# A late S5 input, the tables' transfers on GpSimd's queue and four background steps behind a pair, in a 9-stage fp32 network

## The chip, the cores and the metric

One NeuronCore of a Trainium2 chip runs the whole program. The metric is the device time of one execution in microseconds (us).

## What is computed

A small network runs over 512 tokens of 1024 channels in fp32. The first block has a pooling mixer, a conv-GeGLU layer, windowed attention and a second conv-GeGLU layer, each with a norm ahead of it and one behind. The second block has an S5 mixer and a Mamba-like SSD mixer, each with an MLP behind it. Their inputs are normed and modulated by vectors that come from a condition `c`. In short:

```python
def second_block(x, c, ...):                  # after first_block: pool, ffn, attention, ffn
    ada = silu(c) @ ada_w[i] + ada_b[i]       # six vectors: shift, scale, gate, twice
    h = rmsnorm(x, norm_mix_g) * (1 + scale) + shift
    x = x + gate * s5_mixer(h, ...)           # layer 0; layer 1 has the SSD mixer
    ...                                       # and each layer an MLP, of the same form

def s5_mixer(h, w_in, lam, log_dt, b, c, d, w_glu, b_glu):
    u = h @ w_in
    s_t = exp(lam * dt) * s_(t-1) + b_bar @ u_t          # complex, by group of 16 channels
    y = (c_mat @ s_t).real + d * u
    val, gate = split(gelu(y) @ w_glu + b_glu)
    return val * sigmoid(gate)
```

## The kernel before, in words

The residual `x` lies transposed in SBUF: `xT[k]`, k from 0 to 7, is 128 channels by 512 tokens. Every fp32 product is made of three products of halves: an operand is split into a rounded part (`hi`, or `wh` of a weight) and a remainder (`lo`, `wl`), and lines 218 to 220 add `hi*wh`, `lo*wh` and `hi*wl` in PSUM. ScalarE makes the rounded parts (L203 for weights), VectorE the remainders (L204). Weights come through three buffers `ws`, loaded from SP's queue.

The layers stand in the order pool, ffn0, attn, ffn1, s5, mlp0, ssd, mlp1 and a final norm. Two layers meet in `seam` (L785). For each half of the tokens (256 each) it runs the tail of the old layer, then its chain: `post_add` (L427) makes the post-norm, whose squares are summed on TensorE (`pn`, L303), turned to a root on ScalarE (`sr`, L305), to a reciprocal on VectorE, and spread over all partitions by a second product (L312). `u` (L434) and `x` (L437) follow on VectorE. A step of the new `x`'s squares goes to ScalarE and VectorE (L294, L295).

The new layer's own norm comes in two forms. `PreNorm` runs inside the seam for each half: it waits for all squares of the new `x`, makes the statistics (L303 to L312 again), then `u`, the rounded `h` and its remainder (L388 to L392). `PreScale` is the late form: `h` is the split of `x` times a gain, by `parts` in the same staged loop as `u` and `x` (L418, L419), and the products of the layer are multiplied by the norm's reciprocal root `rs` when they leave PSUM. The two conv-GeGLU layers use `PreScale`, the S5 layer uses `PreNorm` with gain `gs` = (1 + scale) times the weight of the norm, and the shift as an addend. Then the new layer's head computes its first products half by half, and its body the rest over all 512 tokens. In the S5 layer these are `u = h @ w_in`; `u_out` (L1331) copies each from PSUM, permuted, into `usc`, from where it goes through DRAM into `U`.

While a conv-GeGLU layer runs, a `Background` object (L1834) advances generators: `rate` steps behind each of ten pairs of columns, and one behind each of 16 evacuations of the down-projection. What is left is drained behind the body. In ffn0 (rate 5) it computes the tables of the S5 layer (`s5_tables`, `s5_mats`): per group of channels loads `bs` and `cs`, small products on all engines, stores to DRAM (`d_tab`, `d_k`). In ffn1 (rate 3) it computes the condition's vectors by `vecmat` (L466), a vector times a 1024 by 6144 matrix on VectorE: each of 12 blocks of 512 columns takes eight loads `as` of 256 KB into two buffers, one multiply and seven multiply-adds `aa` (L486, L488), then three bf16 parts `ab` by ScalarE with two subtractions between (L498), summed on TensorE. Beside it `s5_toeplitz` reads `d_k` back in shifted form (`tz`, 64 loads), permutes it on ScalarE (`th`, L775, one buffer) and stores it. In the S5 body, `ct` (1 MB each, two buffers) and `vt` (through GpSimd's queue) hold the tables; `dec` and `xs` are small steps on GpSimd.

A scheduler turns the program into an order for each engine; it decides which of the steps above come first on an engine. DMAs are issued in order too: each queue (SP, GpSimd, ScalarE) waits with the first until its buffer is free, and what stands behind it waits as well. `psm` PSUM banks are four, the norm's `psn` one.

## Time and profile before

| what | value |
|---|---|
| median of 3 runs (lowest, highest) | 2488.61 us (2488.39, 2492.14) |
| profiled execution | 2485.38 us |
| its span, first to last instruction | 2483.7 us |
| mean granted TensorE clock | 0.972 |
| busy: TensorE, VectorE, ScalarE, GpSimd | 94%, 69%, 46%, 14% |
| chain that ended last: TensorE, VectorE, DMA, ScalarE, issue | 74%, 12%, 6%, 4%, 3% |

The page shows busy times of the engines as an average over stages. A table by stretch of time then shows where TensorE is not busy, and the timeline of one engine what it waited for there: a row's bracket gives the idle time ahead of an instruction and what ended it. PE is TensorE, DVE is VectorE, ACT is ScalarE, POOL is GpSimd, SP is the queue of SyncE. Line numbers are those of the kernel before.

### The profile page before, as it was taken

To read this page: it belongs to the slowest core of one execution; us is meant where nothing else is said; L and a number is where in the kernel's file an instruction comes from. 1 tells how busy PE (TensorE), PEld (TensorE's weight loads), DVE (VectorE), ACT (ScalarE), POOL (GpSimd) and SP (SyncE) were. 2 spreads that over 40 slices of the span, in tenths; PEclk is the share of its full clock that TensorE was granted. 3 is DMA by queue.
4 is the path that set the end of the run, shared out by engine and by line. 5 is a ranking of instruction groups with operands and counts; after the bars stand their busy time and mean duration, and the time that the engine had idled before them with its cause. 6 is when DMAs were issued, how large, how long until landed. Compare 5 with 4: busy or idle time off the path is not lost.

```text
span 2483.7 us, 33557 instructions
## 1 busy us (share of the span) xinstructions
PE 2340.7 (94%) x12397; PEld 1972.1 (79%) x12397; DVE 1713.8 (69%) x3069; ACT 1142.1 (46%) x2038; POOL 337.9 (14%) x345
## 2 busy tenths in 40 slices
PE   7999999788979999986899999999999999999998
PEld 7877777776778888875878887889878888888888
DVE  6896989678658778786655666666777788633333
ACT  6543535467665444344543433334555554422332
POOL 1001223201200000000110210110143331200110
PEclk9999999889989999997999999999999999999999
DMA  4224443311274555552942455543433332232222
GB/s 122 88 88 140 131 142 103 125 52 51 75 206 134 180 178 165 179 173 68 306 153 77 143 166 191 188 134 92 125 105 99 107 104 80 93 102 94 95 88 72
DMA packets 297780, 311.29 MB, mean 125 GB/s; under 512 B 53569, under 2 KB 251025, under 8 KB 296593
## 3 DMA queue, kind: packets, MB, share of 16 engines
q1 hardware_dynamic: 270033, 278.22, 36.0%
q10 hardware_dynamic: 23680, 17.31, 2.3%
q0 software_dynamic: 3904, 13.63, 1.7%
q8 instruction: 97, 1.59, 0.3%
q14 instruction: 66, 0.54, 0.1%
HBM read 284.92 MB, written 24.18 MB: 124 GB/s over the span
## 4 chain that ended last, share of the span: by engine, by line
PE 74%; DVE 12%; DMA 6%; ACT 4%; issue 3%; SPq 0%; POOL 0%; DVEq 0%; ACTq 0%; POOLq 0%
PE mm L219 22%; PE mm L218 22%; PE mm L220 22%; DMA as<-in_ada_w 3%; DVE wl L204 3%; ACT wh L203 1%; DVE aa L488 1%; PE mm L1642 1%; PE mm L1643 1%; PE mm L1644 1%; PE pb L1712 1%; PE pb L754 1%; DMA tz<-d_k 1%; ACT th L775 1%; DMA d_u<-usc 1%
## 5 line engine op out<-in xcount | busy, mean ns | idle before, releaser
L218 PE MATMUL mm<-h,wh 128*128 128x512 f32 (+1 forms) x1792 | 665.6, 374 | 22.9 <-ACT h L418 7.2
L219 PE MATMUL mm<-h,wh 128*128 128x512 f32 (+1 forms) x1792 | 666.1, 372 | 6.2 <-DVE h L392 3.3
L220 PE MATMUL mm<-h,wl 128*128 128x512 f32 (+1 forms) x1792 | 664.8, 372 | 1.7 <-DVE wl L204 1.7
L203 ACT ACTIVATE wh<-ws 128x1024 fp32r<-128x1024 f32 (+1 forms) x367 | 388.0, 1060 | 563.3 <-PE mm L219 479.6
L204 DVE TENSOR_TENSOR wl<-ws,wh 128x1024 fp32r<-128x1024 f32 (+1 forms) x367 | 466.0, 1272 | 240.7 <-ACT wh L203 234.3
L218 PEld LDWEIGHTS mm<-h,wh 128*128 128x128 f32 x1792 | 346.8, 194 | 81.0 <-issue 8.5
L219 PEld LDWEIGHTS mm<-h,wh 128*128 128x128 f32 x1792 | 347.1, 194 | 63.3 <-DVE h L392 5.4
L220 PEld LDWEIGHTS mm<-h,wl 128*128 128x128 f32 x1792 | 347.3, 194 | 56.3 <-DVE wl L204 2.5
L218 PE MATMUL mm<-hi,wh 128*128 128x512 f32 (+1 forms) x1056 | 369.5, 354 | 9.0 <-ACT wh L203 7.6
L219 PE MATMUL mm<-lo,wh 128*128 128x512 f32 (+1 forms) x1056 | 372.0, 353 | 1.7 <-DVE lo L319 1.7
L220 PE MATMUL mm<-hi,wl 128*128 128x512 f32 (+1 forms) x1056 | 370.8, 353 | 0.8 <-DVE wl L204 0.8
L218 PEld LDWEIGHTS mm<-hi,wh 128*128 128x128 f32 x1056 | 200.6, 190 | 37.3 <-ACT wh L203 8.7
L219 PEld LDWEIGHTS mm<-lo,wh 128*128 128x128 f32 x1056 | 201.4, 191 | 28.5 <-DVE lo L319 2.7
L220 PEld LDWEIGHTS mm<-hi,wl 128*128 128x128 f32 x1056 | 201.2, 191 | 26.8 <-DVE wl L204 1.0
L488 DVE SCALAR_TENSOR_TENSOR aa<-as,cond,aa 128x512 f32<-128x512 f32 x168 | 132.0, 786 | 113.8 <-DMA as<-in_ada_w 112.3
L1266 POOL TENSOR_TENSOR r<-r 128x512 f32<-128x512 f32 x64 | 88.1, 1379 | 671.1 <-ACT r L1262 488.0
L760 POOL TENSOR_TENSOR dd<-ident,s5dg 16x64 f32<-16x64 f32 x16 | 69.4, 4337 | 343.1 <-DVE kt L762 336.1
L319 DVE TENSOR_TENSOR lo<-r,hi 128x512 fp32r<-128x512 f32 x64 | 48.1, 756 | 76.5 <-ACT hi L317 76.4
L1287 DVE SCALAR_TENSOR_TENSOR x<-mm,mod,x 128x512 f32<-128x512 f32 (+1 forms) x76 | 48.9, 662 | 60.6 <-PE mm L220 60.4
L496 ACT ACTIVATE ab<-aa 128x512 bf16<-128x512 f32 x72 | 44.9, 624 | 97.0 <-DVE aa L488 61.7
L317 ACT ACTIVATE hi<-r 128x512 fp32r<-128x512 f32 x64 | 40.4, 631 | 72.3 <-POOL r L1266 72.3
L295 DVE TENSOR_TENSOR acc<-acc,sq 128x256 f32<-128x256 f32 (+1 forms) x148 | 62.0, 432 | 16.4 <-ACT sq L294 11.6
(484 smaller groups left out, 3651.2 us busy)
## 6 DMA issues: line engine op xcount, KB each, us to landing
ws<-in_mlp_w SPq DMA_DIRECT2D x124, 512.0 KB, 4.0
as<-in_ada_w SPq DMA_DIRECT2D x192, 256.0 KB, 3.1
ws<-in_ffn_w_in SPq DMA_DIRECT2D x88, 512.0 KB, 3.8
ws<-in_m_w_in SPq DMA_DIRECT2D x41, 512.0 KB, 3.7
ws<-in_ffn_w_out SPq DMA_DIRECT2D x40, 512.0 KB, 3.5
ws<-in_w_o SPq DMA_DIRECT2D x16, 512.0 KB, 3.4
ct<-d_tab SPq DMA_DIRECT2D x8, 1024.0 KB, 9.5
ws<-in_s_w_glu SPq DMA_DIRECT2D x16, 512.0 KB, 5.8
```

The costliest lines, as they stand in the source:

```text
L203: A.activation(h_, s_, AF.Copy)
L204: V.tensor_tensor(l_, s_, f(h_), ALU.subtract)
L218: T.matmul(ps, wh, xh, start=first, stop=False)
L219: T.matmul(ps, wh, xl, start=False, stop=False)
L220: return T.matmul(ps, wl, xh, start=False, stop=last).ins
L295: V.tensor_tensor(dst, dst, sq[:, a:b], ALU.add)
L319: return hi_, V.tensor_tensor(lo[:, ts], src, f(hi[:, ts]), ALU.subtract)
L488: V.scalar_tensor_tensor(acc, st, col(k), acc, ALU.mult, ALU.add)
L496: A.activation(parts[j], acc, AF.Copy)
L760: G.tensor_tensor(dd, ident[:16, :16].unsqueeze(1).broadcast_to([16, 4, 16]), dg[:, g4].unsqueeze(2).broadcast_to([16, 4, 16]), ALU.mult)
L1266: G.tensor_tensor(r, r, r, ALU.mult)
L1287: V.scalar_tensor_tensor(xT[n][:, ts], ps, md(i, 5, n), xT[n][:, ts], ALU.mult, ALU.add)
```

## The change

1. The S5 layer takes the late input: `PreScale` with the modulated gain. `u_out` multiplies the product by `rs` on VectorE (a new tile `us`) and adds `s5c`, the shift times `w_in`, as the bias of ScalarE's permuting copy. `s5c` is made by a second `vecmat` of two blocks behind the twelve, with its parts permuted as the columns of `w_in` are.
2. These DMAs are issued by GpSimd in place of SP: the `as` loads of layer 0 (96) and of the new product (16 more), the stores `ph` (16) and of zeros to `d_k` (8), the loads `bs` and `cs` (32 each), `tz` (64) and `ct` (8).
3. The second conv-GeGLU layer advances four background steps behind a pair, in place of three.

Two constants of the norms now share a tile.

```diff
     class PreNorm:
...
-            i, m, gname = modulate
-            self.gs = cst.tile([P, KD], F32, tag="gs", bufs=2, name=nm("gs"))
-            c = i * 48 + (m + 1) * 8
-            go = voff[gname] + 8 * i
-            V.scalar_tensor_tensor(self.gs, mod[:, c:c + 8], 1.0, vec[:, go:go + 8], ALU.add, ALU.mult)
+            self.gs = modulated(*modulate)
...
     class PreScale(PreNorm):
-        def __init__(self, norm, eps, gain=None):
-            self.norm, self.eps, self.gain = norm, eps, gain
+        def __init__(self, norm, eps, gain=None, modulate=None):
+            self.norm, self.eps = norm, eps
+            if modulate is not None:
+                gs = modulated(*modulate)
+                self.gain = lambda k: gs[:, k:k + 1]
+            else:
+                self.gain = lambda k: 1.0 if gain is None else vc(gain[0], gain[1] + k)
...
-    def vecmat(pool, W, ncb, col, done):
+    def vecmat(pool, W, ncb, col, done, perm=False, queue=nc.gpsimd):
...
-                nc.sync.dma_start(st, W[k * P:(k + 1) * P, cb * 512:(cb + 1) * 512])
+                queue.dma_start(st, W[k * P:(k + 1) * P, cb * 512:(cb + 1) * 512])
...
+            pv, av = parts, acc
+            if perm:
+                pv = [p_.rearrange("p (a h g) -> p a h g", h=16, g=8) for p_ in parts]
+                av = acc.rearrange("p (a g h) -> p a h g", g=8, h=16)
             for j in range(3):
-                A.activation(parts[j], acc, AF.Copy)
+                A.activation(pv[j], av, AF.Copy)
                 if j < 2:
-                    V.tensor_tensor(acc, acc, parts[j], ALU.subtract)
+                    V.tensor_tensor(av, av, pv[j], ALU.subtract)
...
-        yield from vecmat(pool, I["ada_w_2"][i], 12, lambda k: cond[:, k:k + 1], done)
+        yield from vecmat(pool, I["ada_w_2"][i], 12, lambda k: cond[:, k:k + 1], done,
+                          queue=nc.sync if i else nc.gpsimd)
+        if i == 0 and s5_on:
+            yield from vecmat(pool, I["s5_w_in_2"][0], 2, lambda k: md(0, 0, k),
+                              lambda cb, sums: V.tensor_copy(s5c[:, 4 * cb:4 * cb + 4], sums), perm=True)
...
-            nc.sync.dma_start(dr["tab"][n][:, 512 * i:512 * i + 512], o)
+            nc.gpsimd.dma_start(dr["tab"][n][:, 512 * i:512 * i + 512], o)
...
-                nc.sync.dma_start(bs[:64, e], u[g8].rearrange("g p h -> p g h"))
-                nc.sync.dma_start(bs[64:, e], v[g8].rearrange("g p h -> p g h"))
+                nc.gpsimd.dma_start(bs[:64, e], u[g8].rearrange("g p h -> p g h"))
+                nc.gpsimd.dma_start(bs[64:, e], v[g8].rearrange("g p h -> p g h"))
...
-                nc.sync.dma_start(tz[16 * s:16 * s + 16], dr["kflat"][g8, :, j:j + P].rearrange("g h j -> h g j"))
+                nc.gpsimd.dma_start(tz[16 * s:16 * s + 16], dr["kflat"][g8, :, j:j + P].rearrange("g h j -> h g j"))
...
-                nc.sync.dma_start(ct[n].rearrange("p i g j -> p (i g j)"), dr["tab"][n][:, 2048:])
+                nc.gpsimd.dma_start(ct[n].rearrange("p i g j -> p (i g j)"), dr["tab"][n][:, 2048:])
...
         def u_out(n, ps, span=FULL):
...
-            a = A.activation(usc.rearrange("p (s c) -> p s c", s=8)[:, :, cs], ps.rearrange("p (c s) -> p s c", s=8),
-                             AF.Copy)
+            t = tt("us")[:, :span[1] - span[0]]
+            V.tensor_tensor(t, ps, S_["pre"].rs[:, slice(*span)], ALU.mult)
+            a = A.activation(usc.rearrange("p (s c) -> p s c", s=8)[:, :, cs], t.rearrange("p (c s) -> p s c", s=8),
+                             AF.Identity, bias=s5c[:, n:n + 1])
...
-        return Layer(lambda nxt: PreNorm(nxt, eps2, (0, 0, "norm_mix_g_2")), load, head, body_, tail_,
+        return Layer(lambda nxt: PreScale(nxt, eps2, modulate=(0, 0, "norm_mix_g_2")), load, head, body_, tail_,
...
-            layer = ffn_layer(1, ((0, 8), (8, 16), (16, 22)))
+            layer = ffn_layer(1, ((0, 8), (8, 16), (16, 22)), rate=4)
```

The orders of the two programs differ in three places that matter here. First TensorE between ffn1 and the S5 layer, before: L312 and L303 with `pn` are norms (128x128), `h` are products of the S5 head, 96 to a half, in `mm`.

```order
L220 MATMUL mm_10606<-hi_10066,wl_10030 128x256
L312 MATMUL pn_10356<-dg_10362,ones 128x128 x2
L303 MATMUL pn_10430<-ones,acc_10391 128x128 x2
L312 MATMUL pn_10430<-dg_10436,ones 128x128 x2
L218 MATMUL mm_10793<-h_10414,wh_10752 128x256
...
L220 MATMUL mm_10846<-h_10428,wl_10771 128x256
L312 MATMUL pn_10651<-dg_10657,ones 128x128 x2
L303 MATMUL pn_10708<-ones,acc_10391 128x128 x2
L312 MATMUL pn_10708<-dg_10714,ones 128x128 x2
L218 MATMUL mm_10899<-h_10414,wh_10752 128x256
```

The post-norm of a half (its last row, the first L312 here) is followed at once by the two products of the second norm, and only then by the head's first product. In the changed program (L314, L305, L220 are the former L312, L303, L218):

```order
L222 MATMUL mm_10675<-hi_10162,wl_10126 128x256
L314 MATMUL pn_10468<-dg_10474,ones 128x128 x2
L220 MATMUL mm_10860<-h_10247,wh_10819 128x256
...
L222 MATMUL mm_10917<-h_10261,wl_10838 128x256
L305 MATMUL pn_10720<-ones,acc_10309 128x128 x2
L314 MATMUL pn_10720<-dg_10726,ones 128x128 x2
L220 MATMUL mm_10974<-h_10247,wh_10819 128x256
...
L305 MATMUL pn_10794<-ones,acc_10519 128x128 x2
...
L222 MATMUL mm_11035<-h_10261,wl_10838 128x256
L314 MATMUL pn_10806<-dg_10812,ones 128x128 x2
L220 MATMUL mm_11112<-h_10247,wh_11115 128x512
```

The head's products follow the post-norm of half 0 directly. The post-norm of half 1 stands behind all 96 of them, back to back, and the statistics of the second norm lie among the products of half 1; the last is followed by the first 512-wide product of the body.

Second, ScalarE between attention and ffn1, before: `th` is a table's copy, with the store of it behind, `sr` the root of the first half's post-norm, `h` the rounded inputs.

```order
L775 ACTIVATE th_8151<-tz_8064 128x8x8x16
L776 DMA d_tab<-th_8151 128x1024
L775 ACTIVATE th_8257<-tz_8178 128x8x8x16
L776 DMA d_tab<-th_8257 128x1024
L305 ACTIVATE sr_6963<-pn_6960,eps_88 128x2
L418 ACTIVATE h_6596<-x_95,vec 128x256
```

In the changed program:

```order
L296 ACTIVATE sq_6957<-f_6589 128x256
L307 ACTIVATE sr_6963<-pn_6960,eps 128x2
L795 ACTIVATE th_7789<-tz_7780 128x8x8x16
L796 DMA d_tab<-th_7789 128x1024
L429 ACTIVATE h_6596<-x_95,vec 128x256
L293 ACTIVATE acc_6663<-x_95 128x256
L429 ACTIVATE h_6598<-x_96,vec 128x256
L429 ACTIVATE h_6600<-x_97,vec 128x256
L429 ACTIVATE h_6602<-x_98,vec 128x256
L795 ACTIVATE th_8009<-tz_8000 128x8x8x16
```

Of the copies that stood ahead of `sr`, three now stand behind it, one directly in front of the first `h` and one behind the fourth.

Third, GpSimd in the tables of ffn0, before: `dd` is a small step of each store of tables.

```order
L760 TENSOR_TENSOR dd_3779<-ident,s5dg 16x64
L760 TENSOR_TENSOR dd_3984<-ident,s5dg 16x64
L760 TENSOR_TENSOR dd_4042<-ident,s5dg 16x64
L760 TENSOR_TENSOR dd_4271<-ident,s5dg 16x64
L760 TENSOR_TENSOR dd_4319<-ident,s5dg 16x64
```

In the changed program, at the last groups of channels:

```order
L780 TENSOR_TENSOR dd_3984<-ident,s5dg 16x64
L684 DMA d_tab<-ph_3794 128x512
L684 DMA d_tab<-ph_3800 128x512
L706 DMA cs_4008<-in_s_c_re 128x64
L707 DMA cs_4008<-in_s_c_im 128x64
L706 DMA cs_4008<-in_s_c_im 128x64
L707 DMA cs_4008<-in_s_c_re 128x64
L780 TENSOR_TENSOR dd_4042<-ident,s5dg 16x64
L702 DMA bs_4003<-in_s_b_re 64x8x16
L703 DMA bs_4003<-in_s_b_im 64x8x16
```

The loads `cs` and `bs` of a later group and the stores `ph`, which SP issued, now stand between the `dd` steps, each behind the one ahead of it.

## Rows read from the trace of the kernel before

**Rows 1.** The page's first part: busy time, share and count of each engine.

```profile
PE 2340.7 (94%) x12397; PEld 1972.1 (79%) x12397; DVE 1713.8 (69%) x3069; ACT 1142.1 (46%) x2038; POOL 337.9 (14%) x345
```

**Rows 2.** By stretch: length, busy PE, PEld, DVE, ACT, POOL; granted clock, DMA share, GB/s.

```profile
740.00:1060.00 320.00, 317.53 (x1531) 260.09 (x1532) 254.93 (x386) 142.90 (x196) 1.27 (x2) 0.99 0.51 164
1120.00:1140.00 20.00, 11.25 (x66) 10.58 (x67) 15.75 (x42) 8.54 (x22) 0.00 (x0) 0.63 0.19 65
1140.00:1160.00 20.00, 8.51 (x58) 7.79 (x56) 11.58 (x34) 4.84 (x13) 0.00 (x0) 0.72 0.00 1
```

**Rows 3.** PE's timeline at the S5 seam: start, length, instruction [wait ahead <-what ended it].

```profile
1114.16 0.60 PE L312 MATMUL pn<-dg,ones 128*128 128x128 f32 x4
...
1126.67 1.19 PE L303 MATMUL pn<-ones,acc 128*128 128x128 f32 x4 [11.91 <-DVE acc L295]
...
1128.83 1.20 PE L312 MATMUL pn<-dg,ones 128*128 128x128 f32 x4 [0.96 <-DVE dg L309]
...
1131.13 0.79 PE L218 MATMUL mm<-h,wh 128*128 128x256 f32 x2 [1.11 <-ACT h L391]
...
1145.02 0.60 PE L312 MATMUL pn<-dg,ones 128*128 128x128 f32 x4
...
1155.03 1.20 PE L303 MATMUL pn<-ones,acc 128*128 128x128 f32 x4 [9.40 <-DVE acc L295]
...
1159.50 0.80 PE L218 MATMUL mm<-h,wh 128*128 128x256 f32 x2 [1.11 <-ACT h L391]
...
1173.93 0.40 PE L218 MATMUL mm<-h,wh 128*128 128x512 f32 x1
```

**Rows 4.** DVE's timeline, same place.

```profile
1115.52 1.88 DVE L204 TENSOR_TENSOR wl<-ws,wh 128x1024 fp32r<-128x1024 f32 x1 [0.41 <-ACT wh L203]
1117.31 0.86 DVE L434 SCALAR_TENSOR_TENSOR u<-f,vec,pn 128x256 f32<-128x256 f32 x2
```

**Rows 5.** Timelines of ACT, PE and DVE at the seam from attention to conv-GeGLU.

```profile
733.74 2.03 ACT L775 ACTIVATE th<-tz 128x1024 f32<-128x1024 f32 x1 [5.50 <-DMA d_tab<-th]
...
736.18 0.26 ACT L305 ACTIVATE sr<-pn,eps 128x2 f32<-128x2 f32 x1 [0.40 <-ACT th L775]
...
737.11 1.19 PE L312 MATMUL pn<-dg,ones 128*128 128x128 f32 x4 [6.13 <-DVE dg L309]
...
738.34 0.87 DVE L434 SCALAR_TENSOR_TENSOR u<-f,vec,pn 128x256 f32<-128x256 f32 x2 [1.18 <-PE pn L312]
...
740.14 0.80 PE L218 MATMUL mm<-h,wh 128*128 128x256 f32 x2 [1.84 <-ACT h L418]
...
757.13 0.68 PE L312 MATMUL pn<-dg,ones 128*128 128x128 f32 x4 [0.90 <-DVE dg L309]
```

**Rows 6.** DVE's waits, 740 to 1060 us (us, times, longest); tile `as`, 740 to 1110 us.

```profile
DVE aa L488 <- DMA as<-in_ada_w: 44.4, 36, 3.0
...
L488 DVE SCALAR_TENSOR_TENSOR aa<-as,cond,aa x84: 739/750/756, 771.9 to 1097.6; 128x512 f32<-128x512 f32 x84
...
DMA to landing us min/median/max: 2.6/3.1/7.2
```

**Rows 7.** Tile `vt`, loaded by GpSimd: ns min/median/max of an issue, and landing.

```profile
L1321 POOL DMA_DIRECT2D vt<-d_tab x16: 536/536/722, 1002.4 to 1228.1; - x16
...
DMA to landing us min/median/max: 2.2/3.3/8.6
```

**Rows 8.** PE's waits in the S5 body: us, times, longest.

```profile
PE py L1382 <- DMA ct<-d_tab: 4.6, 2, 4.1
```

**Rows 9.** Timelines of POOL, SP, DVE in the first conv-GeGLU layer; landing of line 682.

```profile
412.74 7.96 POOL L760 TENSOR_TENSOR dd<-ident,s5dg 16x64 f32<-16x64 f32 x1 [15.88 <-DVE kt L762]
...
416.16 0.61 SPq L682 DMA_DIRECT2D bs<-in_s_b_re  x1
...
422.88 0.27 DVE L708 TENSOR_TENSOR b<-bs,s5k 128x128 f32<-128x128 f32 x1
...
DMA to landing us min/median/max: 2.3/2.4/2.5
```

More of the change, by code (lines that the diff above doesn't have):

```diff
@@ L103, in net_kernel @@
     V.memset(one16, 1.0)
-    eps1 = cst.tile([P, 1], F32, name="eps1")
+    eps = cst.tile([P, 2], F32, name="eps")
+    eps1, eps2 = eps[:, 0:1], eps[:, 1:2]
     V.memset(eps1, 1e-6)
-    eps2 = cst.tile([P, 1], F32, name="eps2")
     V.memset(eps2, 1e-5)
@@ L109, in net_kernel @@
     cond = cst.tile([P, KD], F32, name="cond")
+    s5c = cst.tile([P, KD], F32, name="s5c")
+    s5_on = "s5" in parts
     cond_set = []
@@ L360, in behind, with modulated @@
             yield
+    def modulated(i, m, gname):
+        gs = cst.tile([P, KD], F32, tag="gs", bufs=2, name=nm("gs"))
+        c = i * 48 + (m + 1) * 8
+        go = voff[gname] + 8 * i
+        V.scalar_tensor_tensor(gs, mod[:, c:c + 8], 1.0, vec[:, go:go + 8], ALU.add, ALU.mult)
+        return gs
     class PreNorm:
@@ L415, in parts @@
             ts = slice(*span)
-            g = [1.0 if self.gain is None else vc(self.gain[0], self.gain[1] + k) for k in range(KD)]
+            g = [self.gain(k) for k in range(KD)]
             hi, lo = ([h[i][:, ts] for h in self.h] for i in range(2))
@@ L670, in s5_mats @@
         for gb in range(8):
-            nc.sync.dma_start(dr["k"][8 * gb:8 * gb + 8, :, 0].rearrange("g h j -> (g h) j"), zt)
+            nc.gpsimd.dma_start(dr["k"][8 * gb:8 * gb + 8, :, 0].rearrange("g h j -> (g h) j"), zt)
         dg = pool.tile([16, 64], F32, name="s5dg")
@@ L681, in load @@
             for e, (u, v) in enumerate(((bre, bim), (bim, bre))):
-                nc.sync.dma_start(bs[:64, e], u[g8].rearrange("g p h -> p g h"))
-                nc.sync.dma_start(bs[64:, e], v[g8].rearrange("g p h -> p g h"))
+                nc.gpsimd.dma_start(bs[:64, e], u[g8].rearrange("g p h -> p g h"))
+                nc.gpsimd.dma_start(bs[64:, e], v[g8].rearrange("g p h -> p g h"))
             cs = pool.tile([P, 2, 2, 64], F32, tag="cs", bufs=1, name=nm("cs"))
             for e, (u, v) in enumerate(((cre, cim), (cim, cre))):
-                nc.sync.dma_start(cs[:, e, 0], u[g8].rearrange("g h p -> (g h) p"))
-                nc.sync.dma_start(cs[:, e, 1], v[g8].rearrange("g h p -> (g h) p"))
+                nc.gpsimd.dma_start(cs[:, e, 0], u[g8].rearrange("g h p -> (g h) p"))
+                nc.gpsimd.dma_start(cs[:, e, 1], v[g8].rearrange("g h p -> (g h) p"))
             return bs, cs
@@ L1932, in net_kernel @@
     rope_c = {}
-    s5_on = "s5" in names
     ada_on = [any(p in names for p in q) for q in (("s5", "mlp0"), ("ssd", "mlp1"))]
```

## The prediction, made before the run

> **What bounds the kernel now.** I read the page first, then a table by stage, then the single places. TensorE is busy for 2340.7 of 2483.7 us [rows 1], so only its gaps can pay; the question for each part of the change is which gap it touches. In the body of the second conv-GeGLU layer (740 to 1060 us) TensorE is busy for 317.5 of 320 us at a granted clock of 0.99 [rows 2]: nothing can be won there, only lost. At the seam from that layer to the S5 layer it is busy for 11.25 of 20 us and then for 8.51 of 20, at a clock of 0.63 and 0.72 [rows 2]. The timeline shows why [rows 3]. From the second post-norm product of half 0 (1114.16) to the first 512-wide product of the S5 body (1173.93) 59.8 us pass. In them TensorE stands still for 11.91, 0.96 and 1.11 us ahead of half 0, and for 9.40 us and two like the last ahead of half 1. Each long gap is a whole second norm: after the sums `x` are made, all their squares are summed, then the statistics go through TensorE, ScalarE and VectorE, and only then are `u` and `h` formed.
>
> **The seam.** With the late input, `h` is the split of `x` times a gain, known without the second norm. In the new order the head's 96 products of half 0 follow the post-norm directly, then come the post-norm of half 1, both products back to back, and the 96 of half 1; the second norm's statistics lie between these. Step by step, from 1114.16: the first `u` waited until 1117.31, since VectorE did a permuted split of 1.88 us first [rows 4]; the same split stands ahead of it in the new order. From `u` to the first product of a layer that already works this way 1.80 us passed (738.34 to 740.14) [rows 5]: 1119.1. Half 0 took from 1131.13 to 1145.02, 13.9 us, its slow start at the lower clock included [rows 3]: 1133.0. The post-norm of half 1 cannot hide, because nothing is queued between its two products: 2.16 us from the first to the second (1126.67 to 1128.83) [rows 3] and 3.03 us from there to the first product of the new half (737.11 to 740.14) [rows 5]: 1138.2. Half 1 took from 1159.50 to 1173.93, 14.4 us [rows 3]; into it now go the two second norms, four groups of products at 0.6 us as at 1145.02, and a wait of 0.90 us before the last, as at 757.13 [rows 5]: 1155.9. The body starts 18.0 us earlier. VectorE has 24 steps per half (`u`, `x`, `lo`) and 14 additions of squares before the statistics of half 1, some 15 us at the 0.4 us that such a step takes (half of the 0.86 for two `u`) [rows 4]; that ends at 1132.5, beside half 0.
>
> **The price of lateness.** The output of the head must be multiplied by the norm: 12 more VectorE steps, and the bias costs a product of the shift with the weight, two more blocks of the background. The multiplications stand at the layer's start, where VectorE is not the bound (15.75 and 11.58 busy of 20) [rows 2]; if this cover is gone they cost a step's 0.4 to 0.7 us each, 6 us. The blocks are 16 loads and 16 multiply-adds of 0.75 us [rows 6], 12 us, and four subtractions, 3 us at the same price. Eight of the multiply-adds stand beside the layer's tail, as eight did before; only the permuted copies there are new. I take 2 us lost, between 0 and the 15.
>
> **Rate 4.** It puts these blocks, and what the drain did, behind the pairs. TensorE is full there, so the body gives nothing; VectorE decides whether it takes. VectorE is busy for 254.9 of the 320 us [rows 2] and waits 44.4 us for `as` loads [rows 6], which leaves 20.7. Two blocks more need 15 busy and, at 44.4 us for some 90 loads, 8 waiting: just full. But a late multiply-add finds its load landed. I laid the rows of both orders end to end with this trace's durations, each multiply-add waiting until a fixed time after the one two before it. At 3.1 us, the loads' median landing [rows 6], the old order waits some 45, near what was measured. The new one waits 39 us at 3.4, 50 at 3.8 and 88 at 5.0, with totals of 304, 315 and 353, against 326 between first and last multiply-add (771.9 to 1097.6) [rows 6]. GpSimd's loads of the same size landed in 2.2 to 8.6 us, median 3.3 [rows 7], and an issue there takes 0.54 [rows 7]. I take 3.6, the nearest quiet rows (3.3 and a part of an issue): no loss; the ends are 0 and 27.
>
> The Trainium skill ("DMA: Bandwidth & Descriptors", Specifications) gives a first-byte latency of about 1 us on GpSimd's path and about 0.6 on SP's; the medians of rows 6 and 7 differ by less than that. By the page's 0.4 us on top of the present 3.1 the loads would still fit, as an estimate.
>
> **The queue.** SP hands 240 transfers to GpSimd, and 16 new ones go there. What SP's queue delayed is freed: products with `ct` waited 4.6 us for it [rows 8], as its issue stood behind other waits. It now has its own place, though `dec` of a later step stands behind it. I take 2 us gained, between 4.6 gained and 2 lost. At the seam from attention to this layer TensorE waits 6.13 us [rows 5]: ScalarE's `sr` stood behind a table copy `th`, which waited 5.50 us for a store. In the new order `sr` comes three copies earlier, but a copy now stands between it and the first `h`, another behind the fourth. So 6.1 gained or as much as 5.5 lost; 2 us gained, nearer the first, since `sr` gates everything and a copy only some `h`. In the first conv-GeGLU layer the S5 loads `bs` now follow `dd` on GpSimd. In the old trace one such `dd` ran 412.74 to 420.70, `bs` was issued from 416.16 by SP and read at 422.88 [rows 9]. Behind `dd` four issues of 0.6 and a landing of 2.4 [rows 9] end at 425.5: VectorE waits some 2.6 us. One other of the six later groups is as close. I take 2 us lost, between 0 and 8.
>
> The rule of the same page ("Issuing engines are not separate DMA queues") speaks against this part: transfers share 16 engines whoever issues them, so another issuer saves only issue time. By it the 2 us for `ct` fall away; no row here shows `ct` from GpSimd.
>
> **Sum.** 18 + 2 + 2 - 2 - 2 = 18 us. The profiled execution took 2485.4 us around its span of 2483.7, so 2467.4. The median of the runs shown is 3.2 above the profiled one, so the median after is 2470.6. By the same step from 2488.6, 0.2% is 5 us, about what a measurement can tell from no change: faster means below 2483.6, slower above 2493.6.
>
> **Rivals.** First, **VectorE becomes the bound of the body**: loads from GpSimd take 5 us or more under way, as `vt` did at its worst (8.6) [rows 7]. It decides from about 4.2 us on, where the total passes 326. At 5 it costs 27 us: 2497.6, slower. For it: VectorE's thin margin, and every load's release passing through GpSimd's in-order queue. Against: most of the 8.6 is of times with other transfers stacked up, and DMA here is at 0.51 [rows 2]. Chance 0.14.
>
> Second, **the seam keeps one of its gaps**: the additions of squares end late, and half 1's post-norm waits as the second norm did, 9.4 us [rows 3]: 2480. For it: 38 VectorE steps in 15.7 us is tight. Against: half 0's products run at the low clock themselves. Chance 0.12.
>
> Third, **loads behind `dd` hold up the first layer**: at its longest, `dd` and what follows it make each of six `bs` groups 3 us later than VectorE needs it, 18 us: 2488.6, no change. For it: `dd`'s spans are long. Against: only two groups were that close in the old trace. Chance 0.10.
>
> Nor can the late input fail to happen: the order shows it. Of the queue that is open, and it is the 2 and 2 above.
>
> **Numbers.** My forecast has 0.62, with its own range 2460 to 2480: the ends of the attention seam, `ct` and the two prices. The range that should hold 8 in 10 is 2457 to 2487: below, every end above is gained (2460), and 3 us more if the halves' slow starts shorten, as TensorE stands still less before them; above, it takes in the second rival and most of the third, not the first. Faster: 0.62 + 0.12 = 0.74. No change: 0.10, and 0.02 for mixtures. Slower: 0.14.
>
> **What would show it.** In the changed profile: no wait of TensorE above 6 us at the S5 seam, the first 512-wide product some 42 us after the second post-norm product of half 0, not 60; a full TensorE in the body with VectorE busier by 15 us; the wait for `sr` at the attention seam smaller; no wait for `ct`. It is wrong if the body shows TensorE waiting for `u` or VectorE waiting far over 50 us for `as`, or if new waits on `bs` or `cs` appear before 480 us.

## The result, and the profile after

The changed kernel took 2470.86 us (median of 4 runs, 2469.30 to 2474.89) against 2488.50 for the kernel before beside it (4 runs): a ratio of 0.9940, 95% interval 0.9926 to 0.9954. The forecast was 2470.6. The total came out as forecast; most of its terms did not, and their errors cancelled, which was luck. The page after, its first part and the transfers of `ct`:

```profile
PE 2336.3 (95%) x12421; PEld 1970.3 (80%) x12421; DVE 1722.3 (70%) x3089; ACT 1153.0 (47%) x2046; POOL 482.5 (20%) x617
...
ct<-d_tab POOLq DMA_DIRECT2D x8, 1024.0 KB, 5.9
```

TensorE is busy for 4.4 us less than before [rows 1] in a span that is 16.2 us shorter (2467.5), so 11.8 us of the gain are idle time and 4.4 are busy time, at a mean granted clock of 0.976 where it was 0.972.

Where the time went is read from nine marks on TensorE's timeline, in this and in every later run: its first product, the first 512-wide product of ffn0, the last product of ffn0's tail, the last score of attention, the first 512-wide product of ffn1, the last product of ffn1's tail, the first 512-wide product of the S5 body, the last table product `py`, and its last instruction. The table gives by how much each stage between two marks is longer (+) or shorter than in the kernel before, in us of the profiled executions; the first counts from the start of the span to the second mark.

| run | start | ffn0 | scores | to ffn1 | ffn1 | S5 seam | S5 tables | rest | sum |
|---|---|---|---|---|---|---|---|---|---|
| the change | +4.1 | +2.4 | -8.2 | -12.6 | +4.9 | -13.3 | +7.6 | -1.0 | -16.2 |
| 1 late input alone | -0.1 | -0.6 | -0.6 | -0.1 | +2.8 | +23.4 | +4.3 | +4.3 | +33.6 |
| 2 queues alone | +6.2 | +2.6 | -5.3 | -11.4 | -3.8 | -1.3 | +5.8 | +3.6 | -3.4 |
| 3 rate 4 alone | +1.3 | -0.1 | 0.0 | -0.9 | +3.8 | -4.7 | -0.9 | +2.6 | +1.1 |
| 4 late input and rate 4 | +1.8 | 0.0 | 0.0 | -0.4 | +8.3 | -16.2 | +2.6 | +2.1 | -1.7 |
| 5 first `bs`, `cs` on SP | -0.3 | +3.2 | -8.7 | -8.0 | +5.8 | -13.7 | +8.0 | +3.9 | -9.8 |
| 6 `ct` on SP | +5.8 | +2.4 | -5.3 | -12.4 | +6.4 | -13.6 | +2.8 | +1.7 | -12.1 |
| 7 `bs`, `cs` on SP | 0.0 | -0.7 | -1.6 | -8.9 | +3.7 | -13.5 | +9.5 | +0.6 | -10.8 |
| 8 `tz` alone on GpSimd | -0.9 | -0.5 | -1.2 | -11.9 | +4.6 | -1.2 | +0.5 | -1.0 | -11.6 |
| 9 only `tz`, `as` on GpSimd | +1.4 | -0.4 | -0.5 | -8.1 | +1.5 | -13.1 | +3.3 | +3.6 | -12.3 |
| 10 rate 5 | +4.4 | +2.4 | -8.2 | -11.8 | +37.0 | -16.7 | +7.6 | +2.4 | +17.2 |
| 11 as 9, rate 5 | +0.5 | -0.1 | -0.1 | -8.7 | +32.4 | -15.9 | +3.4 | +3.2 | +14.7 |
| 12 half the head | +5.4 | +2.8 | -5.6 | -12.4 | +5.8 | | | +3.7 | -8.0 |

No edit touches the last stage, of 1215 us, yet it lies between -1.0 and +4.3: in a stage of that length differences under some 5 us say nothing in a single profile, and single sums differ from the medians by as much. `ffn1` is no better: runs 2 and 8, which leave its rate and its blocks alone, have -3.8 and +4.6. Other stages repeat well over runs that share an edit. `ffn0` lies between +2.4 and +3.2 in the six runs whose later `bs` and `cs` come from GpSimd (the change, 2, 5, 6, 10, 12), and between -0.7 and 0.0 in the other seven. In run 12 the mark ahead of the S5 body is another place, so seam and tables are taken together: -7.7, where the change has -5.8.

**The S5 seam.** TensorE's timeline, as in [rows 3]:

```profile
1104.83 0.68 PE L314 MATMUL pn<-dg,ones 128*128 128x128 f32 x4
...
1109.74 0.80 PE L220 MATMUL mm<-h,wh 128*128 128x256 f32 x2 [4.23 <-ACT h L429]
...
1124.39 0.61 PE L305 MATMUL pn<-ones,acc 128*128 128x128 f32 x4
...
1125.96 0.68 PE L314 MATMUL pn<-dg,ones 128*128 128x128 f32 x4 [0.97 <-DVE dg L311]
...
1128.49 0.80 PE L220 MATMUL mm<-h,wh 128*128 128x256 f32 x2 [1.84 <-ACT h L429]
...
1143.94 0.61 PE L305 MATMUL pn<-ones,acc 128*128 128x128 f32 x4
...
1148.00 0.68 PE L314 MATMUL pn<-dg,ones 128*128 128x128 f32 x4 [2.97 <-DVE dg L311]
...
1151.22 0.80 PE L220 MATMUL mm<-h,wh 128*128 128x512 f32 x1 [2.54 <-DVE us L1357]
```

The two long waits are gone, as the late input was to do. Up to the first product of half 1 the steps are those of the prediction, and their sizes too: 23.7 us from the post-norm's second product (1104.83 to 1128.49), forecast 24.0. Then half 1 took 22.7 us and not 17.7: two waits, 2.97 for `dg` and 2.54 for `us`, stand ahead of the body. VectorE's timeline tells what was late:

```profile
1143.70 3.76 DVE L206 TENSOR_TENSOR wl<-ws,wh 128x1024 fp32r<-128x1024 f32 x2 [0.19 <-ACT wh L205]
1147.38 0.16 DVE L308 RECIPROCAL sr<-sr 128x2 f32<-128x2 f32 x1
1147.57 0.48 DVE L311 TENSOR_SCALAR dg<-ident,sr 128x128 f32<-128x128 f32 x2
1147.97 0.42 DVE L1357 TENSOR_TENSOR us<-mm,rsx 128x256 f32<-128x256 f32 x1
1148.95 1.89 DVE L206 TENSOR_TENSOR wl<-ws,wh 128x1024 fp32r<-128x1024 f32 x1 [0.56 <-ACT wh L205]
1150.75 1.40 DVE L1357 TENSOR_TENSOR us<-mm,rsx 128x256 f32<-128x256 f32 x4
```

The reciprocal `sr` stood behind two permuted splits of weights, 3.76 us; `dg` and the first `us` follow, and a third split lies ahead of the other `us`. By stretch, with the columns of [rows 2], the ffn1 body and two parts of the seam (half 0, half 1):

```profile
743.50:1060.00 316.50, 312.53 (x1489) 254.09 (x1488) 259.80 (x389) 142.09 (x188) 55.32 (x103) 1.00 0.55 176
1109.70:1124.40 14.70, 14.08 (x97) 13.58 (x98) 12.18 (x34) 7.84 (x22) 0.00 (x0) 0.83 0.44 147
1128.50:1151.20 22.70, 16.70 (x112) 16.04 (x112) 19.18 (x40) 14.98 (x24) 0.00 (x0) 0.80 0.21 70
```

The body of ffn1 is a little less full than before: 312.5 of 316.5 us (first row), where [rows 2] have 317.5 of 320. In half 1 TensorE is busy for 16.7 of 22.7 us, at a clock of 0.80, in half 0 for 14.1 of 14.7 at 0.83.

**The start.** Nothing of it was in the prediction. GpSimd's instructions from 2.19 us on, and TensorE's first:

```profile
2.19 0.90 POOL L702 DMA_DIRECT2D bs<-in_s_b_re  x1
...
4.46 0.30 POOL L850 TENSOR_SCALAR_AFFINE_SELECT band<-band 128x128 f32<-128x128 f32 x1
4.70 0.69 POOL L703 DMA_DIRECT2D bs<-in_s_b_re  x1
...
8.13 0.53 POOL L850 TENSOR_SCALAR_AFFINE_SELECT band<-band 128x128 f32<-128x128 f32 x2
```

```profile
9.46 0.45 PE L146 MATMUL mm<-ident,rt 128*128 128x128 f32 x1 [9.46 <-POOL band L850]
...
15.57 0.77 PE L902 MATMUL mm<-band,xr 128*128 128x128 f32 x2 [5.66 <-DVE xr L887]
```

The eight loads of the first group, of 0.5 to 0.9 us each to issue, stand among and ahead of the steps that make the pooling bands; before, GpSimd made these without a break from 2.46 us on. The first product waits 9.46 us (7.80 before), the first product with a band another 5.66. Before, the first of these followed at once, at 8.04 us, and a later one waited 1.47.

**ffn0.** VectorE now waits for `bs`, which it did not before:

```profile
DVE b L728 <- DMA bs<-in_s_b_im: 3.2, 1, 3.2
```

This wait and one of 0.8 us are in the change and in runs 2, 5, 6, 10 and 12 (3.1 to 3.5 and 0.7 to 0.8 us), and in no other run.

**The scores.** TensorE's busy time from the end of ffn0 to the last score, before and after (columns of [rows 2]):

```profile
483.10:651.92 168.82, 143.74 (x719) 117.93 (x718) 133.20 (x303) 112.89 (x312) 23.19 (x15) 0.89 0.14 44
489.58:650.21 160.63, 138.45 (x722) 113.46 (x721) 131.76 (x301) 110.20 (x305) 21.23 (x13) 0.93 0.14 44
```

Of the 8.2 us gained 5.3 are busy time, for as many products, at a granted clock of 0.93 where it was 0.89.

**The S5 tables.** The wait for `ct` [rows 8] is gone; others took its place. TensorE's waits there (us, times, longest), the longest of them with what VectorE did ahead of it, and GpSimd's timeline ahead of the second:

```profile
PE py L1405 <- DVE xs L1396: 5.6, 3, 3.9
...
PE py L1405 <- POOL xs L1395: 2.5, 1, 2.5
```

```profile
1234.57 0.77 PE L1405 MATMUL py<-xs,ct 128*128 128x128 f32 x2 [3.95 <-DVE xs L1396]
```

```profile
1231.19 0.69 DVE L1386 TENSOR_TENSOR t<-pv,rot 128x512 f32<-128x512 f32 x1 [1.01 <-ACT sw L1371]
1231.80 0.68 DVE L1387 TENSOR_TENSOR sw<-sw,rot 128x512 f32<-128x512 f32 x1
1232.40 2.02 DVE L1396 TENSOR_TENSOR xs<-st,sw 128x504 f32<-128x504 f32 x1
```

```profile
1206.88 1.98 POOL L1419 TENSOR_TENSOR gl<-yf,gh 128x512 fp32r<-128x512 f32 x1 [5.07 <-ACT gh L1418]
1208.81 0.10 POOL L1395 MEMSET xs<- 128x8 f32 x1
```

At 1232.40 VectorE made `xs` only behind `t` and `sw` of the next step, and one product waited 3.95 us for it. This one exchange in VectorE's order, with a wait of 3.9 to 4.0 us, is in all six runs with `ct` on GpSimd (the change, 2, 5, 7, 10, 12) and in none of the others. The clearing of `xs` at 1208.81 stood behind `gl`, and one product waited 2.48 us for it (1208.97); run 6, with `ct` on SP, has the same wait, so it is not `ct`'s. No product waits for `dec`. By stretch the tables before, after and in run 6:

```profile
1173.93:1260.75 86.82, 76.57 (x517) 69.72 (x516) 54.53 (x64) 45.81 (x64) 17.18 (x31) 0.98 0.86 271
1151.22:1245.61 94.39, 81.81 (x515) 74.51 (x516) 57.43 (x71) 49.19 (x67) 24.63 (x44) 0.92 0.78 238
1157.27:1246.91 89.64, 78.42 (x515) 71.01 (x516) 53.58 (x71) 49.08 (x67) 21.93 (x38) 0.96 0.82 250
```

Of the 7.6 us that were lost 5.2 are busy time of TensorE, for as many products, at a granted clock of 0.92 where it was 0.98.

**The background in ffn1.** VectorE's waits for `as`, and the landing of the loads from GpSimd's queue [rows 6 has both from SP's]:

```profile
DVE aa L500 <- DMA as<-in_ada_w: 45.2, 33, 3.6
DVE aa L500 <- DMA as<-in_s_w_in: 5.1, 5, 2.0
...
DMA to landing us min/median/max: 2.8/3.1/5.2
```

### The profile page after: what moved, and what is told of

Same layout as the page of the kernel before. It is cut to its first block, busy times and chain, and to the rows that moved or that the text cites. A ratio compares the mean times of both kernels' runs of the same rounds, so it can differ in the third digit from the quotient of the medians.

```text
span 2467.5 us, 33702 instructions
## 1 busy us (share of the span) xinstructions
PE 2336.3 (95%) x12421; PEld 1970.3 (80%) x12421; DVE 1722.3 (70%) x3089; ACT 1153.0 (47%) x2046; POOL 482.5 (20%) x617
## 4 chain that ended last, share of the span: by engine, by line
PE 65%; DVE 15%; DMA 8%; issue 7%; ACT 4%; POOL 1%; SPq 0%; ACTq 0%; DVEq 0%; POOLq 0%
PE mm L221 19%; PE mm L220 19%; PE mm L222 19%; DMA as<-in_ada_w 5%; DVE wl L206 3%; DVE aa L500 2%; ACT wh L205 1%; PE mm L1664 1%; PE mm L1665 1%; PE mm L1666 1%; PE pb L1734 1%; PE pb L774 1%; DVE u L959 1%; PE py L1405 1%; DVE tg L965 1%
## 5 line engine op out<-in xcount | busy, mean ns | idle before, releaser
L220 PE MATMUL mm<-h,wh 128*128 128x512 f32 (+1 forms) x1792 | 666.6, 374 | 30.4 <-ACT h L429 13.9
L220 PEld LDWEIGHTS mm<-h,wh 128*128 128x128 f32 x1792 | 346.2, 194 | 89.4 <-ACT h L429 15.4
L220 PE MATMUL mm<-hi,wh 128*128 128x512 f32 (+1 forms) x1056 | 370.8, 356 | 9.5 <-ACT wh L205 9.3
L220 PEld LDWEIGHTS mm<-hi,wh 128*128 128x128 f32 x1056 | 202.0, 192 | 37.0 <-ACT wh L205 10.5
L512 ACT ACTIVATE ab<-aa 128x512 bf16<-128x512 f32 x78 | 51.8, 664 | 124.8 <-DVE aa L500 86.9
L495 POOL DMA_DIRECT2D as<-in_ada_w x96 | 51.6, 538 | 244.6 <-DVE aa L500 120.1
L780 POOL TENSOR_TENSOR dd<-ident,s5dg 16x64 f32<-16x64 f32 x16 | 62.5, 3909 | 85.2 <-DVE kt L782 79.2
```

The lines of the kernel that those rows point to most:

```text
L220: T.matmul(ps, wh, xh, start=first, stop=False)
L495: queue.dma_start(st, W[k * P:(k + 1) * P, cb * 512:(cb + 1) * 512])
L512: A.activation(pv[j], av, AF.Copy)
L780: G.tensor_tensor(dd, ident[:16, :16].unsqueeze(1).broadcast_to([16, 4, 16]), dg[:, g4].unsqueeze(2).broadcast_to([16, 4, 16]), ALU.mult)
```

## The experiments

Each was timed beside the kernel before, whose medians were 2489.6 us (runs 1 to 4), 2489.3 (5 to 8) and 2491.0 (9 to 12); the ratio is to these. Theory A is the prediction's sum, theory B what the trace of the change suggested.

**1. The late input alone.** All transfers on SP, rate 3; of the diff only the parts on `PreScale`, `u_out` and `s5c` are kept.

> The late S5 input alone: every transfer back on SP, three background steps behind a pair. Theory A (the sum of the prediction): the seam is worth 18 us and its price 2, so about 2472 us. Theory B (the trace of the change: the seam gave 13.4 us from the second post-norm product of half 0 to the first 512-wide product, and the stretch of attention about 20, which the late input has no part in): 13 us less, and 4 to 8 more for the two extra blocks, which at three steps behind a pair fall into the drain beside the layer's tail: 2479 to 2484 us, with attention unchanged.

Measured: 2518.97 us, ratio 1.0113 (1.0098 to 1.0128). Both theories failed. TensorE's waits between 1075 and 1230 us, and two of them:

```profile
PE pn L484 <- ACT ab L512: 36.1, 7, 13.6
```

```profile
1127.63 0.26 PE L484 MATMUL pn<-one,ab 128*128 128x1 bf16 x4 [11.85 <-ACT ab L512]
...
1145.78 0.26 PE L484 MATMUL pn<-one,ab 128*128 128x1 bf16 x4 [13.60 <-ACT ab L512]
```

L484 is the sum of a `vecmat` block on TensorE. At rate 3 the two blocks of `s5c` are drained behind the layer, and their sums stand in TensorE's order ahead of the S5 head. TensorE did nothing else while VectorE went through those of the 16 loads and multiply-adds that were left when the layer ended. So the late input loses 29 us by itself at rate 3; with rate 4 (run 4) that loss is gone.

**2. The queues alone.**

```diff
-                nc.sync.dma_start(tz[16 * s:16 * s + 16], ...)
+                nc.gpsimd.dma_start(tz[16 * s:16 * s + 16], ...)
```

and so for `as`, `ct`, `bs`, `cs`, `ph` and the zeros.

> The queues alone: the same transfers issued by GpSimd, early S5 input, three steps. Theory A: about 2 us less than before, 2486 us. Theory B: attention and its seam gain some 20 us, since SP hands over the shifted table loads that stood among the weight loads; the start loses 4 (first loads of the S5 tables ahead of the pooling bands on GpSimd) and the first conv-GeGLU layer 2: 2474 to 2478 us.

Measured: 2480.71 us, 0.9962 (0.9949 to 0.9975). Theory B was right on where the gain lies, 16.6 us between ffn0 and ffn1, and its total was missed by 2.7 us: 6.2 were lost at the start, 2.6 in ffn0, and 5.8 in the S5 tables, which it did not have. Half of the change's gain is the queues', where the prediction gave them 2 us.

**3. Rate 4 alone.**

> Four background steps behind a pair alone. Theory A: no difference, within 3 us of before, as TensorE is full in the layer's body. Theory B: the same inside the body; at its end the drain is shorter, so 0 to 4 us less; attention and the S5 layer unchanged.

Measured: 2484.97 us, 0.9978 (0.9969 to 0.9988): 4.6 us less, with an interval from 3.0 to 7.7. Theory A's 3 us and theory B's 0 to 4 just reach into it, but both had an unchanged body. TensorE's longest wait in ffn1:

```profile
PE mm L218 <- DVE u L939: 7.9, 3, 4.0
```

In the body TensorE waits for `u` of VectorE, as it does in run 4 (4.6 us), where `as` also comes from SP; with `as` on GpSimd this wait is 0.6 us in the change and at most 2.3 in the others at rate 4. The layer is longer by 3.8 us, and the seam behind it, with a shorter drain, shorter by 4.7.

**4. The change without its queues.**

> The changed program with every transfer back on SP. Theory A: 2472 us or less. Theory B: the queue's net gain (20 at attention, minus 4 at the start and 2 in the first layer) is lost: about 2482 to 2486 us; first product of TensorE at 7.8 us again instead of 9.5.

Measured: 2486.99 us, 0.9988 (0.9978 to 0.9997). The queues' gain is lost, as theory B had it, 1 us above its upper end; the first product came at 8.1 us. The seam is shorter by 16.2 us, and ffn1 longer by 8.3, of which 3.8 come with rate 4 alone (run 3). Runs 2 and 4 add up to -11.5 us of the median, the change has -17.6; in the profiles the largest part of that difference, 6.7 us, lies in the last stage (+3.6 and +2.1, against -1.0), which no edit touches.

**5. The first group's loads on SP.**

```diff
         def load(gb):
+            q = nc.gpsimd if gb else nc.sync
...
-                nc.gpsimd.dma_start(bs[:64, e], u[g8].rearrange("g p h -> p g h"))
+                q.dma_start(bs[:64, e], u[g8].rearrange("g p h -> p g h"))
```

> The changed program, with only the first group's eight loads (bs, cs) back on SP. If these issues ahead of the pooling bands on GpSimd cost the start, TensorE's first product comes at 7.8 us and not at 9.5, the body of the first conv-GeGLU layer starts 4 us earlier, and the time falls by about 4 us, to 2467. If the start is late for another reason (SP's second half of the input, issued 1 us later), the start moves by 1 us or not at all.

Measured: 2475.89 us, 0.9953 (0.9938 to 0.9968). The cause of the late start is shown: first product at 7.8 us, the start as before (-0.3). The time did not fall: the way to ffn1 gained 8.0 in place of 12.6, and the last stage lost 3.9. TensorE's order in attention is another one than in the change (run 7); whether the new orders took the 4 us back or the last stage's scatter did is not shown.

**6. `ct` on SP.**

> The changed program, with the eight table loads ct back on SP. If the S5 body is longer because ct stands ahead of dec and xs on GpSimd and waits for the products of the step before, the 5 to 7 us that the stretch from its first to its last table product lost come back, less the 4.6 us that TensorE waited for ct before: 2466 to 2471. If the body is longer for the clock alone, nothing changes but the wait for ct comes back: 2475.

Measured: 2474.62 us, 0.9949 (0.9933 to 0.9966). TensorE's waits in the S5 body:

```profile
PE py L1405 <- DVE xs L1396: 3.0, 3, 1.3
```

The tables are longer by 2.8 us, not 7.6, so some 4.7 us of the loss go with `ct` on GpSimd: 1.4 in waits (for `xs` 5.6 fell to 3.0, while one of 1.7 for `dec` came back) and 3.4 in TensorE's busy time, at a clock of 0.96 and not 0.92. The stage repeats: with late input it is 7.6 to 9.5 us longer with `ct` on GpSimd (the change, 5, 7, 10) and 2.6 to 4.3 with `ct` on SP (1, 4, 6, 9, 11). No wait for `ct` came back, so its going in the change was not due to GpSimd. The total did not follow: the start, the scores and the rest went the other way.

**7. All `bs` and `cs` on SP.**

> The changed program, with all bs and cs loads back on SP. If loads behind the dd steps hold up the first conv-GeGLU layer, as the prediction said, its body is shorter by the 2.4 us that it lost, beside the 4 at the start: about 2464.5. If only the start counts, about 2467, the same as with the first group alone.

Measured: 2479.92 us, 0.9961 (0.9946 to 0.9977). ffn0 is shorter by 0.7 us where the change lost 2.4 and run 5 3.2, and the waits for `bs` are gone, so the loads behind `dd` are the loss in ffn0, as predicted. But the gain of the scores is gone, and with it the profit. TensorE's order from the first score to the last, with buffer numbers left out, goes with it: it is one and the same in the kernel before and in runs 1, 3, 4, 7, 8, 9 and 11 (422 products), another in the change and in runs 2, 6, 10 and 12 (428 products), and a third in run 5 (414 products). With the first order that stage is shorter by 0 to 1.6 us, with the others by 5.3 to 8.7. The other orders come in just those runs whose later `bs` and `cs` are issued by GpSimd. Their last issue ends at 431 us, before the first score (490 us and later), which speaks for the order as the cause and not the queue; the order was not moved by itself, and why the planner (the scheduler that makes these orders) chooses so was not tried.

**8. `tz` alone on GpSimd, on the kernel before.**

> The kernel before, with the 64 shifted loads tz alone moved to GpSimd. If the gain of the attention stretch is SP's queue freed of them, most of the 17 us that the queues alone gained between the first score product and the body of the second conv-GeGLU layer is here, with no loss at the start: 2471 to 2475. If it comes from the order in which the copies th stand, or from the as loads leaving SP, less than half of it: 2480 or more.

Measured: 2479.82 us, 0.9954 (0.9936 to 0.9971). TensorE's waits from 652 to 760 us, before and with `tz` moved:

```profile
PE pn L312 <- DVE dg L309: 7.0, 2, 6.1
PE mm L218 <- ACT f L1144: 3.0, 3, 2.1
PE mm L218 <- ACT wh L203: 2.0, 1, 2.0
```

```profile
PE pn L312 <- DVE dg L309: 2.2, 2, 1.3
PE mm L218 <- ACT f L1144: 0.9, 2, 0.7
PE mm L218 <- ACT wh L203: 0.6, 2, 0.5
```

The stretch from the last score to ffn1 gains 11.9 us, the change 12.6: that gain comes with `tz`. The scores gain 1.2, so the first case of the expectation was right on one part of its 17 us and wrong on the other. TensorE waits for `dg` 2.2 us in place of 7.0, for `f` and `wh` 1.5 in place of 5.0, and its granted clock over the stretch is 0.98 where it was 0.92. Two things came with the edit, and the run does not part them: SP's `ws` loads have no `tz` between them any more, and in ScalarE's order three copies `th` stand behind `sr`, as in the change, so that `dg` no longer waits behind the copy of [rows 5].

**9. Only `tz` and `as` on GpSimd.** The change with `ct`, `bs`, `cs`, `ph` and the zeros on SP.

> The changed program with only tz and the as loads on GpSimd; ct, bs, cs and the two kinds of stores back on SP. If the parts add up as the single runs showed them (attention some 14 us gained by tz alone, the seam 13, no loss at the start, none in the first conv-GeGLU layer, none in the S5 tables, 5 lost in the second conv-GeGLU layer), it gains 20 to 22 us: about 2467, better than the change. If the order of the other work shifts as in the two runs with bs and cs moved back, the gain at attention shrinks by what is won elsewhere: 2473 to 2478.

Measured: 2475.14 us, 0.9934 (0.9912 to 0.9955). The start, ffn0 and most of the S5 tables came back, but the scores' gain went, and the way to ffn1 gained 8.1 only. The ratio is that of the change (0.9940) within the intervals. No run beats the change beyond them.

**10. Rate 5.**

> The changed program with five background steps behind a pair. All 112 multiply-adds then stand in the layer's body and none beside its tail. If VectorE is the bound of the body by now (the prediction's rival), the body grows by 5 us or more and the time with it: 2475 or more. If VectorE still has room, the tail gains what the eight multiply-adds and the permuted copies cost there, 0 to 3 us: 2468 to 2471.

Measured: 2506.02 us, 1.0064 (1.0042 to 1.0086). TensorE's waits in ffn1, and its busy time from 760 to 1060 us (columns of [rows 2]):

```profile
PE pn L484 <- ACT ab L512: 21.5, 10, 11.9
```

```profile
760.00:1060.00 300.00, 279.57 (x1318) 223.29 (x1317) 228.14 (x337) 120.21 (x159) 54.46 (x102) 0.97 0.55 174
```

One step more and the layer takes 37 us more than before. TensorE waits for `ab` ahead of the blocks' sums, as in run 1: the first rival's price, through another door than `u`. VectorE itself is busy for only 228 of these 300 us; what fills its time is the wait for loads, from 760 to 1060 us:

```profile
DVE aa L500 <- DMA as<-in_ada_w: 60.5, 40, 3.4
```

In the change this wait is 45.2 us.

**11. Only `tz` and `as`, rate 5.**

> The two last in one: only tz and as on GpSimd, five steps. If both are as the parts say, 2464 to 2468; if the body is bound by VectorE, 5 us above the run with four steps.

Measured: 2504.52 us, 1.0050 (1.0031 to 1.0068), 29 us above run 9. The same loss; the queues of the other transfers have no part in it.

**12. Half the head.** `S5_HEAD` is 1 and not 2.

> The changed program with a head of the S5 layer half as large (48 products a half, two PSUM banks held and not four). If the late norm costs the seam its last 2.5 us because all four banks wait for it, TensorE's wait for us ahead of the first 512-wide product goes away; the wait for dg stays or grows, as fewer products stand ahead of the statistics. Seam shorter by 2 us, or longer by up to 5 if the post-norm of half 1 now waits for its squares.

Measured: 2477.66 us, 0.9948 (0.9930 to 0.9965). TensorE's longest waits from 1111 to 1250 us:

```profile
PE mm L220 <- ACT h L429: 6.1, 2, 4.2
PE py L1405 <- DVE xs L1396: 4.6, 2, 4.0
PE pv L1382 <- DMA U<-d_u: 3.3, 1, 3.3
```

A wait for `us` is not among TensorE's waits any more, which speaks for the four banks as what held the body back. The wait for `dg` of the second norm (2.97 us in the change) went too, against the expectation: the norm's last product now stands among 512-wide products of the body. But one wait of 3.3 us for `U` came in. Seam and tables together are 1.9 us shorter than in the change, less than one profile can tell from nothing.

## Why the prediction was right, and where not

**The seam: mechanism right, size off by 4.7 us.** 13.3 gained, 18.0 forecast. The step that failed is "into it now go the two second norms, four groups of products at 0.6 us, and a wait of 0.90 us". The products were there; the wait was 5.5 us, for `dg` and then `us`. The 0.90 came from a seam whose weights are not permuted. A split there takes 1.23 us. Here permuted splits, of 1.88 us each by [rows 4], stand ahead of the reciprocal, and the body's first product waits until `us` empties a bank. That an evacuation now depends on the norm was counted as work ("they cost a step's 0.4 to 0.7 us each") and not as a wait on the path. Of the prediction's stretch, from the post-norm's product to the body, 46.4 us were measured, 42 forecast, 59.8 before. With half the head both waits are gone (run 12).

**The price of lateness and rate 4: each mis-sized, and not two terms.** "I take 2 us lost" for the blocks is not confirmed, and no run settles it: ffn1 is 4.5 us longer in run 4 than in run 3, which has rate 4 without the blocks; in the change it is 8.7 longer than in run 2 and 0.3 longer than in run 8, neither of which has them. The end given, 15, holds all of these. A price that the sum had nowhere shows in the S5 tables: with late input and `ct` on SP they are 2.6 to 4.3 us longer (five runs), with early input -0.9 and +0.5 (runs 3 and 8); what makes it was not traced. "No loss" for rate 4 failed in the body when it came alone: TensorE waited 7.9 us for `u` (run 3), the sign named for a wrong forecast, and the shorter drain gave the time back at the seam. In the change that wait is 0.6 us. What the prediction missed is that lateness and rate hang together: without rate 4 the blocks cost 23 us at the seam (run 1). Loads from GpSimd landed after 3.1 us at the median, where 3.3 and a part of an issue were taken; VectorE waited 50.3 us for `as`, and the hand-laid order had 39 at 3.4 and 50 at 3.8. VectorE was busy for 12 us more in ffn1 (282.3 before, 294.3 after), 15 forecast.

**The queue: attention right in place and far too small, `ct` of the wrong sign.** SP handed over 256 transfers, not the 240 of the text; GpSimd's count grew by 272 with the 16 new ones. For the seam to ffn1 2 us were taken of the 6.1 that were the end; 12.6 came. The wait for `dg` fell by 4.8 in run 8, as the 6.1 foresaw; the waits for `f` and `wh`, 3.5 us, and the clock were in no term. The step "a copy now stands between it and the first `h`" cost nothing: that `h` waited 1.14 us for `x` when the copy had ended. The scores' 8 us were in no term either; they go with an order of the planner, which the prediction did not follow for that stage. For `ct`, "it now has its own place, though `dec` of a later step stands behind it. I take 2 us gained" failed in both halves. The wait for `ct` is gone in run 6 too, with `ct` back on SP, and in runs 1 and 3, where no transfer moved, so GpSimd did not earn it. And some 4.7 us were lost, not by `dec`, for which no product waits in the change, but with an exchange in VectorE's order ahead of one product and a lower granted clock. For ffn0 2 us were taken, 2.4 came, by waits for `bs` of 3.2 and 0.8 us, and run 7 shows them to be `bs` and `cs` behind `dd`. The start, 4.1 us, was left out altogether: the prediction followed each moved load past `dd`, and not past what GpSimd does first.

**Issue time and first byte.** By the Trainium skill ("DMA: Bandwidth & Descriptors", "Issuing engines are not separate DMA queues") only issue time is saved by another issuer. The runs do not speak against it: the 64 issues of `tz` took a median of 0.43 us on SP, some 27 us by an estimate from these two numbers, more than the 11.9 that run 8 gained, and by the rule the gain for `ct` falls away, as it did. The rule does not have the orders that came with each move. Of the longer first byte on GpSimd's path that the Trainium skill gives ("DMA: Bandwidth & Descriptors", Specifications) the medians show nothing: 3.1 us there, 3.1 from SP [rows 6].

**The rivals.** VectorE as the bound did not come true in the change. It showed at rate 4 with `as` on SP, by waits for `u` (runs 3 and 4), and at rate 5 by the blocks' sums, where VectorE's waits for loads and not its work grew (run 10). The seam kept none of its long gaps. Loads behind `dd` cost 2.4 us, not 18.

**The sum.** Forecast -18; the stages gave +4.1, +2.4, -8.2, -12.6, +4.9, -13.3, +7.6 and -1.0, that is -16.2 in the profiled execution and -17.6 in the medians. Some 21 us gained ahead of ffn1, where 2 were expected, paid for what the start, ffn1, the seam and the tables gave less. The total was met because errors of both signs cancelled: the number was luck, and only the seam's mechanism, the place of the gain at attention and the loss in ffn0 were foreseen.

## What to carry to other kernels

A DMA that changes its queue is to be followed on both queues from the first instruction on: what it leaves is the gain (`tz`), what now stands behind it is the price (the pooling bands, `bs` behind `dd`), and the first microseconds of the program belong to it. Before a norm is made late, look for whatever the multiplication now gates (banks, and the products that need them), and for the work that a bias brings: if its products stand in TensorE's order ahead of the next layer, the work must be done by then. Under a planner each edit also changes orders elsewhere; compare those listings stage by stage, for every engine, before a gain or a loss is put down to the edit itself, and run the parts alone before giving a total to any of them.

## What was not expected

A background step too few or too many costs more than the whole seam is worth: with all transfers on SP the late input takes 2519 us at rate 3 and 2487 at rate 4, and the change takes 2506 at rate 5 and 2471 at rate 4. In both cases TensorE stood still ahead of products of 0.06 us, up to 13.6 us at a time, since these stand in its order ahead of the layer's or the next layer's products. And four runs (5, 6, 7 and 9) that each mended a loss of the change came out no faster than it beyond the intervals; in two of them (7 and 9) TensorE's order in attention is again that of the kernel before, and 6.6 and 7.7 us of the scores' 8.2 are gone.
